# The output projection of one token block by seven products, and four reorderings around the norms

## The chip, the cores and the metric

The kernel runs on one core of a Trainium2 chip. The metric is device time in microseconds (us) of one execution; a time is the median of several runs. PE is the matrix engine, PEld its weight loads, DVE the vector engine, ACT the scalar engine, POOL GpSimd, and SP the engine that here only issues DMAs. ACT, DVE, SP and POOL each take their instructions in the order in which the kernel's program queues them.

## The reference

2112 tokens (2048 of a prompt, 64 of a sample) pass one layer, all in float32:

```
h = rms_norm(x, g_pre);  proj = h @ w_in                  # ten groups of 1024 columns
yA = (silu(zA) * bA * conv3(cA * vA)) @ w_a_out
o  = gated linear attention over chunks of 64 tokens (8 heads of 128)
yB = (rms(o) * g_onorm * silu(zB)) @ w_b_out
merged = sigmoid(gA) * yA + sigmoid(gB) * yB
out = merged @ w_o
x = x + rms_norm(out, g_post)
gate = sigmoid(rms_norm(x, g_ple) @ w_ple_gate)
x = x + (p @ w_ple_proj) * gate
```

## The kernel before

**Tiling.** The tokens are cut into three blocks (0, 1, 2) of 704, each with two halves ("segs") of 352. Activations lie features by tokens: a tile of 128 features x 704 tokens is a `rt()` of one ring of 52 tiles. A float32 product is made of three matmuls in a split format: each operand is cut into `hi` (an ACT cast) and `lo` (a DVE subtraction, `split`), and hi x hi, hi x lo and lo x hi are summed in PSUM. The low parts of the weights are written to DRAM the first time (`lows`, in `split_w`) and loaded later instead of computed.

**Seven products.** Most projections treat two blocks of output columns, two halves of the contraction and the two halves of tokens as a 2 x 2 block product in the Strassen-Winograd form: seven block products in place of eight, with sums of weight blocks (S1 to S4, kept in DRAM by `keep_sum` or `prepare_sums`) and of activation blocks (T1 to T4, `sums_of`). `sgroup` does so for one pair of columns. `in_turn` does it for a whole 1024 x 1024 matrix, one product after the other, each over four rows g of blocks (12 matmuls each); `operand_of` forms the next product's operand from the raw tiles, in place, one k after each row. Block 0 uses plain `gemms` for W_A, W_B and W_O. Block 1 uses `in_turn` for W_A and W_B (`merge_in_turn`) and `gemms` for W_O (`final_out`), for which `made` splits the merged tiles. Block 2 uses `in_turn` for all three (`out_in_turn`).

**The order of the work.** PE's work is written out as one sequence. Slower side work (norms, attention steps, operands) hangs on `hooks`, a list popped once after each product or row: `spread_out` says how many steps of a generator belong to each hook, and places them, on ACT and DVE, behind the latest PSUM evictions (`copies`, `adds`, by `behind_all`). `placed` puts matmuls of side work behind PE's last main matmul. Instructions are then put into each engine's queue by a scheduler that goes by priority and dependencies.

**PSUM.** Eight banks: five in `psg` (`ps_gemm`, written pg in the profile) and three in `psa` (`ps_attn`, written pa).

**Between blocks.** While W_O of block b is worked, `operands` scales the x of block b+1 and makes its seven operands, one k pair at a time. Then `gates` starts for block b+1: eight groups, seven of them (`LEAD`) at once, with block b's `final_norm` on their hooks: the root mean square (`rms`: column sums L614 on PE, a power on POOL L587, a broadcast L598 on PE, a copy on ACT L624), eight steps that make x, a second root mean square, and eight that make h. The eighth gate group is taken up by `path_b` at head 0. In the last block the norm runs by halves, on hooks of W_O, of the second projection `ple` (L1028 to L1030, evicted at L1035) and of the gate matmuls.

**The start.** Block 0's `ple` and its row sums come first; then `plain_group` takes k by k what `first_operands` has split, and between two k's `next_k` runs one operand step and one step of block 1's `ple` (`second_ple`).

Of the kernel before, what the change touches and what calls it, by code (L numbers as in the profile page):

```python
# [78 lines left out]
IN_TURN = (("A11", "B11"), ("A12", "B21"), ("S2", "T2"), ("S3", "T3"), ("A22", "T4"), ("S1", "T1"), ("S4", "B22"))  # L79
# [3 lines left out]
def hybrid_step(  # L83
# [113 lines left out]
    lows, turn = {}, [0]  # L197
# [11 lines left out]
    def split_w(raw, key=None):  # L209
# [9 lines left out]
        if key is not None:  # L219
            lows[key] = dram.tile([P, 4, P], F32, tag=f"lo{key}", name=nm("low"), bufs=1)  # L220
            SP.dma_start(lows[key], lo.bitcast(F32))
# [12 lines left out]
    last, hooks, copies, adds = [None], [], [None], [None]  # L234
# [33 lines left out]
    def keep_sum(name, i1, s):  # L268

        sums.setdefault(i1, {})[name] = dram.tile([P, 4, P], F32, tag=f"{name}_{i1}", name=nm(name), bufs=1)  # L270
        SP.dma_start(sums[i1][name], s)
        return split_w(s, (i1, name))
# [179 lines left out]
    def operand_of(raw, name, k):  # L452

        (b11, b12), (b21, b22) = ([half(raw[i], h) for h in range(2)] for i in (k, k + KH))
        if name == "T2":
            V.tensor_tensor(b11, b12, b11, ALU.subtract)
            t = hf()
            V.tensor_tensor(t, b22, b11, ALU.subtract)
            V.tensor_tensor(b12, b22, b12, ALU.subtract)
            V.tensor_tensor(b21, b21, t, ALU.subtract)  # L460
            return narrow(t)
        return narrow(dict(B11=b11, B21=b21, T3=b12, T4=b21, T1=b11, B22=b22)[name])

    def in_turn(stages, operand):

# [4 lines left out]
        def prepare(i, k):  # L470
            if i < len(todo):
                st, n = todo[i]
                made.setdefault(i, []).append(operand_of(st["raw"], IN_TURN[n][1], k))

        for i, (st, n) in enumerate(todo):
            if n == 0:
                st["mid"], st["bank"] = [], {}
            xs = made.pop(i)
            for g in range(KH):
                i1, i2 = st["idx"] + g, st["idx"] + KH + g  # L480
                with tc.high_priority():
                    hi, lo = kept_w(i1, i2, IN_TURN[n][0], IN_TURN[n][0] in st["anew"])
                start = n in (0, 2, 3, 5)
                if start:
                    st["bank"][g] = ps_gemm()
                ps = st["bank"][g]
# [6 lines left out]
                if n == 0:  # L493
# [3 lines left out]
                u2, p7 = half(st["mid"][g], 0), half(st["mid"][g], 1)  # L497
                if n == 1:
                    st["sink"](g, 0, 0, ps, None)
                elif n == 2:  # L500
                    V.tensor_tensor(u2, u2, ps, ALU.add)
                elif n == 3:
                    with tc.high_priority():
                        A.copy(p7, ps)
                elif n == 4:
                    st["sink"](g, 1, 0, u2, ps)
                elif n == 5:
                    p5 = hf()
                    with tc.high_priority():
                        A.copy(p5, ps)  # L510
                    V.tensor_tensor(p7, p7, p5, ALU.add)
                    st["sink"](g, 1, 1, u2, p7)
                elif n == 6:
                    st["sink"](g, 0, 1, u2, ps)
# [103 lines left out]
    def rms(acc, out, segs):  # L618
# [4 lines left out]
        for sg, col in zip(segs, cols):  # L623
            A.copy(out[:, cols_of(sg)], spread(col, sg["n"]))  # L624
# [56 lines left out]
    def operands(hc, rs, load):  # L681

        for i in range(KH):
            pair = []
            for k in (i, i + KH):
                pair.append(load(k))
                scaled_x(pair[-1], k, rs)
            hc["B11"].append(narrow(half(pair[0], 0)))
            sums_of(hc, pair)
            hi, lo = split_rt(pair[1])  # L690
            hc["B21"].append((half(hi, 0), half(lo, 0)))
            hc["B22"].append((half(hi, 1), half(lo, 1)))
            yield
# [292 lines left out]
    def path_b(bl, hc, first, kept, fills, hs):  # L986
# [25 lines left out]
    def ple(bl, ph, kept, held=None, shared=False):  # L1012

        for j in range(KB):
            if held is not None:
                hi, lo = held[j]
            else:
                raw = wp.tile([P, 4, P], F32, tag="raw", name=nm("raw"), bufs=5)[:, :2, :]
                SP.dma_start(raw, w_ple[j])
                with tc.high_priority():  # L1020
                    hi = wp.tile([P, 4, P], F32R, tag="hi", name=nm("hi"))[:, :2, :]
                    lo = wp.tile([P, 4, P], F32R, tag="lo", name=nm("lo"))[:, :2, :]
                    split(raw, hi, lo)
            t = rt()
            for s in bl["segs"]:
                pp, c = ps_attn()[:, :HN], cols_of(s)
# [11 lines left out]
            else:  # L1038
                kept["p", j] = spill("p", j)
                G.dma_start(kept["p", j], t)  # L1040
            with behind_all((copied,) if hooks else ()):
# [45 lines left out]
    def merge_in_turn(a, kept, mg, made):  # L1087
# [9 lines left out]
        def sink_b(g, c, h, x, y):  # L1097
# [3 lines left out]
            made(j, h)  # L1101

        def loads(idx, n):
# [13 lines left out]
            dict(idx=W_A, raw=a, sink=sink_a, anew=("A11", "A12")),  # L1117
            dict(idx=W_B, raw=ob, sink=sink_b, anew=("A11", "A12")),
        ], loads

    def final_out(segs, mg, xo, acc, late):

        for j, pss in enumerate(gemms(W_O, mg, segs, True, late)):
# [10 lines left out]
    def out_in_turn(mg, xo, acc):  # L1134
        xo.extend(rt() for _ in range(KB))
        begun = set()

        def sink(g, c, h, x, y):
            v = half(xo[g + c * KH], h)
            into(v, x, y)  # L1140
            sum_squares(int(h in begun), v, half(acc, h), HN)
            begun.add(h)

        return dict(idx=W_O, raw=mg, sink=sink, anew=())

    def final_norm(bl, segs, xo, acc, h2, kept):
# [15 lines left out]
        yield from rms(acc, rs, segs)  # L1162
        for j in range(KB):
# [4 lines left out]
            sum_squares(j, xj, acc2[:, c], n)  # L1168
            yield
        yield from rms(acc2, rs2, segs)  # L1170
        for j in range(KB):
            xj = xo[j][:, c]
# [5 lines left out]
            t = rt()  # L1178
            V.scalar_tensor_tensor(t[:, c], xj, g_ple[:, j : j + 1], rs2[:, c], ALU.mult, ALU.mult)
# [263 lines left out]
```

## Time and profile before

| | |
|---|---|
| median of 3 runs | 2653.56 us (2651.12 to 2655.82) |
| the profiled execution, its own time | 2661.89 us |
| its span, first to last instruction | 2660.2 us |
| mean clock granted to PE | 0.994 |
| DMA | 732.90 MB, mean 276 GB/s |
| HBM read, written | 524.66 MB, 205.01 MB |

How to read it: a busy share is an average over stages with different limits, so what an edit is worth is read in its stage. Matmuls are pipelined, and the duration of one (324 ns for 352 columns) is about twice the distance between two starts, so time is counted from start to start. Likewise DVE and ACT operations overlap their successors a little. A wait is put down to the releaser that came last.

### The profile page before, as it was taken

Reading aid. Unit: us, or ns where it says so; the run is one execution under the profiler, and the core shown is the slowest. Engines: PE = TensorE matmul, PEld = TensorE weight load, DVE = VectorE, ACT = ScalarE, POOL = GpSimd, SP = SyncE. Lnnn points to the kernel's source line nnn. Section 1 sums busy time; section 2 is a strip of 40 time slices with the busy share of each in tenths; the row PEclk is TensorE's granted clock in tenths of the full one; section 3 lists DMA queues with packets and bytes.
Section 4 is the critical chain, followed back from the end, with each engine's and each line's share of the span. In section 5 each row is a group of like instructions: output and inputs, shape, how many; then the busy total and the mean of one; then the engine's idle time right before and its main releaser. Section 6 shows DMA issues by size and latency. Waiting matters only on the chain.

```text
span 2660.2 us, 47727 instructions
## 1 busy us (share of the span) xinstructions
PE 2624.7 (99%) x16748; PEld 2606.2 (98%) x16748; DVE 1688.3 (63%) x3281; ACT 1474.9 (55%) x2872; POOL 351.3 (13%) x649
## 2 busy tenths in 40 slices
PE   7999999999999999999999999999999999999999
PEld 7999999999999999999999999999999999999998
DVE  7688888888676555556645577553365554347856
ACT  5665665554335544566655565554566654445664
POOL 1000000200441210101112210021000000001011
PEclk9999999999999999999999999999999999999999
DMA  7677787988997988676689988698866678889965
GB/s 288 218 275 271 247 281 259 314 310 289 373 348 268 352 299 270 225 230 221 223 290 363 389 308 290 191 349 312 273 218 220 216 227 264 273 277 313 298 210 177
DMA packets 359793, 732.90 MB, mean 276 GB/s; under 512 B 43808, under 2 KB 46400, under 8 KB 359552
## 3 DMA queue, kind: packets, MB, share of 16 engines
q1 hardware_dynamic: 322560, 586.10, 65.6%
q0 software_dynamic: 36704, 143.70, 14.9%
q8 instruction: 132, 2.16, 0.3%
q14 instruction: 109, 0.89, 0.1%
q10 hardware_dynamic: 288, 0.05, 0.0%
HBM read 524.66 MB, written 205.01 MB: 274 GB/s over the span
## 4 chain that ended last, share of the span: by engine, by line
PE 91%; DMA 3%; DVE 3%; issue 2%; ACT 1%; POOL 0%; SPq 0%; ACTq 0%; DVEq 0%; POOLq 0%
PE pg L357 19%; PE pg L359 19%; PE pg L358 19%; PE pg L525 5%; PE pg L523 5%; PE pg L524 5%; PE pg L491 3%; PE pg L490 3%; PE pg L492 3%; DMA raw<-S 2%; PE pa L963 1%; PE pa L927 1%; PE pa L917 1%; PE pa L965 1%; PE pa L916 1%
## 5 line engine op out<-in xcount | busy, mean ns | idle before, releaser
L357 PE MATMUL pg<-r,hi 128*128 128x352 f32 x3304 | 1094.0, 331 | 1.9 <-ACT hi L214 1.5
L358 PE MATMUL pg<-r,hi 128*128 128x352 f32 x3304 | 1069.1, 324 | 0.0
L359 PE MATMUL pg<-r,lo 128*128 128x352 f32 x2356 | 763.0, 324 | 3.7 <-DMA lo<-low 3.7
L214 ACT CAST hi<-raw 128x512 fp32r<-128x512 f32 x708 | 435.5, 619 | 572.6 <-PE pg L358 202.0
L357 PEld LDWEIGHTS pg<-r,hi 128*128 128x128 f32 x3304 | 623.6, 189 | 6.1 <-issue 2.2
L358 PEld LDWEIGHTS pg<-r,hi 128*128 128x128 f32 x3304 | 623.5, 189 | 0.1
L359 PEld LDWEIGHTS pg<-r,lo 128*128 128x128 f32 x2356 | 444.0, 188 | 4.4 <-DMA lo<-low 4.3
L359 PE MATMUL pg<-r,s 128*128 128x352 f32 x948 | 307.3, 324 | 2.4 <-DMA s<-low 2.4
L524 PE MATMUL pg<-r,hi 128*128 128x352 f32 x896 | 289.8, 324 | 0.4 <-DVE r L184 0.4
L523 PE MATMUL pg<-r,hi 128*128 128x352 f32 x896 | 289.7, 324 | 0.4 <-ACT r L184 0.3
L525 PE MATMUL pg<-r,lo 128*128 128x352 f32 x756 | 244.6, 324 | 0.1
L184 ACT CAST hi<-raw 128x512 fp32r<-128x512 f32 (+1 forms) x242 | 145.8, 612 | 163.8 <-PE pg L358 45.5
L184 DVE TENSOR_TENSOR r<-r,r 128x352 fp32r<-128x352 f32 (+3 forms) x274 | 169.5, 636 | 65.6 <-ACT r L184 64.9
L184 DVE TENSOR_TENSOR lo<-raw,hi 128x512 fp32r<-128x512 f32 (+1 forms) x242 | 162.7, 678 | 72.9 <-ACT hi L184 61.3
L184 ACT CAST r<-r 128x352 fp32r<-128x352 f32 (+3 forms) x274 | 150.3, 578 | 67.5 <-DVE r L666 17.5
L491 PE MATMUL pg<-r,hi 128*128 128x352 f32 x560 | 181.9, 325 | 0.4 <-DVE r L184 0.3
L359 PEld LDWEIGHTS pg<-r,s 128*128 128x128 f32 x948 | 178.7, 189 | 3.2 <-DMA s<-low 3.2
L490 PE MATMUL pg<-r,hi 128*128 128x352 f32 x560 | 178.5, 325 | 0.1
L184 ACT CAST hi<-s 128x512 fp32r<-128x512 f32 x160 | 99.0, 619 | 139.0 <-PE pg L358 119.7
L523 PEld LDWEIGHTS pg<-r,hi 128*128 128x128 f32 x896 | 168.7, 188 | 1.4 <-ACT r L184 1.1
L524 PEld LDWEIGHTS pg<-r,hi 128*128 128x128 f32 x896 | 168.8, 188 | 0.8 <-DVE r L184 0.6
L371 ACT COPY hf<-pg 128x352 f32<-128x352 f32 x354 | 155.8, 448 | 6.8 <-PE pg L359 6.3
(365 smaller groups left out, 4088.4 us busy)
## 6 DMA issues: line engine op xcount, KB each, us to landing
raw<-w_blk SPq DMA_DIRECT2D x590, 256.0 KB, 3.9
lo<-low SPq DMA_DIRECT2D x404, 256.0 KB, 3.9
raw<-S SPq DMA_DIRECT2D x392, 256.0 KB, 4.0
low<-lo SPq DMA_DIRECT2D x346, 256.0 KB, 3.7
s<-low SPq DMA_DIRECT2D x304, 256.0 KB, 3.9
S<-s SPq DMA_DIRECT2D x160, 256.0 KB, 3.3
r<-w_blk POOLq DMA_DIRECT2D x48, 256.0 KB, 7.5
S<-r POOLq DMA_DIRECT2D x48, 256.0 KB, 6.2
```

What stands on the lines that cost most here:

```text
L184: return A.copy(hi, src).ins, V.tensor_tensor(lo, src, hi.bitcast(F32), ALU.subtract).ins
L214: A.copy(hi, raw)
L357: add(hi[:, k, :], xhi, start=start and k == 0, stop=False)
L358: add(hi[:, k, :], xlo, start=False, stop=False)
L359: last[0] = add(lo[:, k, :], xhi, start=False, stop=k == KH - 1).ins
L371: copied = A.copy(got[n], ps[bank])
L490: add(hi[:, k, :], xhi, start=start and k == 0, stop=False)
L491: add(hi[:, k, :], xlo, start=False, stop=False)
L492: last[0] = add(lo[:, k, :], xhi, start=False, stop=k == KH - 1).ins
L523: T.matmul(ps, hi[:, k % 4, :], xhi[:, c], start=k == ks[0], stop=False)
L524: T.matmul(ps, hi[:, k % 4, :], xlo[:, c], start=False, stop=False)
L525: last[0] = T.matmul(ps, lo[:, k % 4, :], xhi[:, c], start=False, stop=k == ks[-1]).ins
```

## The change

1. W_O of block 1 goes through `in_turn` with an order of its own (`IN_TURN_LATE`): S1 T1 comes third, then S2 T2 into a bank of `psa`, S4 B22, S3 T3, A22 T4. `made` and its splits go. The squares of its output are taken in `final_norm`, on hooks of the gates.
2. `operands` has three steps for a pair in place of one and asks for the next pair's x ahead (`early`); they hang on the 28 hooks of that W_O.
3. From block 1 on the stores of sums and low parts are issued by POOL. The eighth gate group is taken up at head 4.
4. At the start `next_k` runs the projection ahead of the operand step, two steps of it the first time; the operand step goes behind the evictions, and three of `second_ple`'s halves use `ps_gemm`.
5. In the last block the squares of x lag by one tile, h's scalings run one tile ahead of its splits, the broadcasts are copied by DVE (`hasten`), the low parts of `w_ple` are loaded from DRAM, the last product's additions go behind that copy (`ahead`), and the counts of steps per hook change. Block 0's counts change as well.

```diff
+IN_TURN_LATE = (
+    ("A11", "B11", "p1"), ("A12", "B21", "c11"), ("S1", "T1", "p5"), ("S2", "T2", "u2"), ("S4", "B22", "c12"),
+    ("S3", "T3", "p7"), ("A22", "T4", "c21"),
+)
...
-            SP.dma_start(lows[key], lo.bitcast(F32))
+            stores[0].dma_start(lows[key], lo.bitcast(F32))
...
-        SP.dma_start(sums[i1][name], s)
+        stores[0].dma_start(sums[i1][name], s)
...
                 if start:
-                    st["bank"][g] = ps_gemm()
-                ps = st["bank"][g]
+                    other = what == "u2" and st["order"] is IN_TURN_LATE
+                    st["bank"][g] = [ps_attn()[:, :HN] if other else ps_gemm(), st["bank"].get(g)]
+                ps, held = st["bank"][g]
...
+            if hasten:
+                ahead[:] = [V.tensor_copy(out[:, cols_of(sg)], spread(col, sg["n"])).ins]
+            else:
+                A.copy(out[:, cols_of(sg)], spread(col, sg["n"]))
...
-    def operands(hc, rs, load):
+    def operands(hc, rs, load, early=False):
+        pair = None
         for i in range(KH):
-            pair = []
-            for k in (i, i + KH):
-                pair.append(load(k))
-                scaled_x(pair[-1], k, rs)
+            pair = pair or [load(k) for k in (i, i + KH)]
+            for k, xk in zip((i, i + KH), pair):
+                scaled_x(xk, k, rs)
             hc["B11"].append(narrow(half(pair[0], 0)))
+            yield
             sums_of(hc, pair)
+            yield
...
+            pair = [load(k) for k in (i + 1, i + 1 + KH)] if early and i + 1 < KH else None
             yield
...
-            if not (first and hd == 0):
+            if hd > 0 if first else hd == NH // 2:
                 next(fills, None)
...
-                    lo = wp.tile([P, 4, P], F32R, tag="lo", name=nm("lo"))[:, :2, :]
-                    split(raw, hi, lo)
+                    lo = low_tile()[:, :2, :]
+                    A.copy(hi, raw)
+                    SP.dma_start(lo.bitcast(F32), lows["p", j])
...
-                pp, c = ps_attn()[:, :HN], cols_of(s)
+                pp = ps_gemm() if spare and j in (1, 3, 5) and s is bl["segs"][1] else ps_attn()[:, :HN]
...
+        if squares:
+            for j in range(KB):
+                sum_squares(j, xo[j], acc, BN)
+                if j % 2:
+                    yield
...
-            sum_squares(j, xj, acc2[:, c], n)
+            for i in (j,) if not bl["last"] else (j - 1,) if 0 < j < KB - 1 else (j - 1, j) if j else ():
+                sum_squares(i, xo[i][:, c], acc2[:, c], n)
...
     def next_k():
-        run(ops, 1)
         with placed():
-            run(second_ple, 1)
+            run(second_ple, 2 if len(hs) == 2 else 1)
+        with behind_all(copies):
+            run(ops, 1)
...
+        if bi == 1:
+            stores[0] = G
...
+            stages.append(out_in_turn(mg, xo, acc, bl["last"]))
...
+                if nxt and (idx, n) == (W_B, 6):
+                    hc = new_operands()
+                    ops = operands(hc, spread_all(cols), partial(load_x, nxt), True)
+                    spread_out((ops, (0, 1, 0, 1, 0, 1, 0) * KH))
...
-                    spread_out((norms[0], (0, 0, 1, 0, 1, 1, 1, 1)))
+                    spread_out((norms[0], (1, 0, 1, 1, 1, 0, 1, 0)))
...
-            spread_out((norm, (0, 1, 0, 1) + (0, 1, 0) * KB + (1, 0, 1) + (0, 1) * KB))
+            start = (0, 1, 0, 1) + (0, 1, 0) * KB if first else (1, 1, 1, 1, 0, 1, 0, 1) + (0, 1) * KB
+            spread_out((norm, start + (0, 1, 0, 1) + (0, 1) * KB))
...
-            spread_out((norms[0], (2, 2, 1, 1, 1, 3, 3, 2)), (norms[1], (0,) * 6 + (1, 1) + (2, 2, 2, 2, 1, 0, 1, 3, 3, 2)))
+            spread_out((norms[0], (2, 2, 1, 0, 1, 1, 4, 4)), (norms[1], (0,) * 6 + (1, 1) + (1, 2, 2, 2, 1, 1, 1, 3, 3, 2)))
```

More of the change, by code (lines that the diff above doesn't have):

```diff
@@ L231, in load_w @@
         return parts
-    last, hooks, copies, adds = [None], [], [None], [None]
+    last, hooks, copies, adds, ahead = [None], [], [None], [None], []
     def placed():
@@ L1132, in final_out, with out_in_turn, final_norm @@
         yield
-    def out_in_turn(mg, xo, acc):
-        xo.extend(rt() for _ in range(KB))
+    def out_in_turn(mg, xo, acc, last):
+        stage = dict(idx=W_O, order=IN_TURN if last else IN_TURN_LATE, raw=mg, anew=())
+        if last:
+            xo.extend(rt() for _ in range(KB))
         begun = set()
         def sink(g, c, h, x, y):
-            v = half(xo[g + c * KH], h)
+            if not last and c == 0 and h == 0:
+                xo.append(rt())
+            v = half((xo if last or c == 0 else stage["mid"])[g + c * KH * last], h)
             into(v, x, y)
[L1141 to L1146, printed above, removed]
+            if last:
+                sum_squares(int(h in begun), v, half(acc, h), HN)
+                begun.add(h)
+        stage["sink"] = sink
+        return stage
+    def final_norm(bl, segs, xo, acc, h2, kept, squares=False):
         c = slice(segs[0]["off"], segs[-1]["off"] + HN)
```

134 lines of the change are left out of this document (74 added, 60 removed).

## The prediction

> **What bounds the kernel now.** I read the page's busy table and chain, then busy time by stage, then the matmul queue's waits stage by stage.
>
> ```profile
> span 2660.2 us, 47727 instructions
> PE 2624.7 (99%) x16748; PEld 2606.2 (98%) x16748; DVE 1688.3 (63%) x3281; ACT 1474.9 (55%) x2872; POOL 351.3 (13%) x649
> ...
> PE 91%; DMA 3%; DVE 3%; issue 2%; ACT 1%; POOL 0%; SPq 0%; ACTq 0%; DVEq 0%; POOLq 0%
> ```
>
> PE is busy for 99% of the span and is 91% of the chain. A matmul not issued is therefore worth its pitch, and besides that only the places count where PE is held up or runs at a lower clock. The stages (columns: stretch, length, then PE, PEld, DVE, ACT, POOL busy, PE clock, DMA share, GB/s):
>
> ```profile
> 33.00:36.50 3.50, 3.50 (x14) 3.27 (x13) 3.50 (x6) 1.58 (x5) 0.00 (x0) 0.52 1.04 410
> ...
> 57.00:61.00 4.00, 4.00 (x17) 4.00 (x16) 3.42 (x6) 1.10 (x3) 0.33 (x1) 0.57 0.93 300
> 920.50:924.00 3.50, 3.50 (x15) 3.50 (x14) 0.00 (x0) 0.99 (x3) 1.51 (x2) 0.52 1.05 401
> 1064.00:1067.50 3.50, 3.50 (x14) 3.50 (x13) 0.52 (x1) 1.41 (x2) 0.00 (x0) 0.51 0.70 249
> ...
> 1591.00:1646.00 55.00, 54.90 (x334) 53.34 (x333) 46.00 (x101) 34.70 (x75) 5.33 (x10) 1.00 0.89 301
> 1646.00:1661.00 15.00, 14.33 (x90) 13.38 (x89) 12.15 (x27) 5.93 (x13) 1.60 (x3) 1.00 0.80 296
> 1661.00:1722.00 61.00, 61.00 (x381) 61.00 (x380) 29.35 (x43) 28.82 (x52) 3.75 (x7) 1.00 0.58 186
> 1722.00:1785.00 63.00, 59.54 (x366) 58.18 (x366) 32.69 (x51) 38.90 (x71) 14.22 (x24) 0.97 0.97 351
> ...
> 2441.00:2495.00 54.00, 54.00 (x335) 53.59 (x334) 47.15 (x100) 34.33 (x75) 7.44 (x14) 1.00 0.95 332
> 2570.00:2576.00 6.00, 5.92 (x20) 5.92 (x21) 5.93 (x15) 4.19 (x12) 0.00 (x0) 0.50 0.18 44
> ```
>
> The undisturbed stage 2441 to 2495 gives the pitch: 54.00 us / 335 matmuls = 0.161 us for 352 columns. At clock 0.51, 14 matmuls filled 3.5 us, 0.25 us each; a half-clock stretch of about 3.4 us thus costs 3.4 x (1 - 0.161/0.25), 1.2 us, to 3.4/2 = 1.7 us. I use 1.5.
>
> PE's hold-ups that the change can reach (the bracket is the idle time and its releaser):
>
> ```profile
> 30.06 0.81 PE L427 MATMUL pg<-r,hi 128*128 128x352 f32 x2 [1.22 <-ACT r L184]
> 32.17 0.43 PE L428 MATMUL pg<-r,hi 128*128 128x352 f32 x1 [1.30 <-DVE r L184]
> 50.11 0.43 PE L1028 MATMUL pa<-r,r 128*128 128x352 f32 x1 [1.75 <-ACT r L1035]
> 56.19 0.43 PE L1028 MATMUL pa<-r,r 128*128 128x352 f32 x1 [1.96 <-ACT r L1035]
> ...
> 1063.19 0.43 PE L359 MATMUL pg<-r,lo 128*128 128x352 f32 x1 [2.25 <-DMA lo<-low]
> ...
> 1656.46 0.43 PE L523 MATMUL pg<-r,hi 128*128 128x352 f32 x1 [0.27 <-ACT r L184]
> 1657.24 0.43 PE L524 MATMUL pg<-r,hi 128*128 128x352 f32 x1 [0.36 <-DVE r L184]
> ...
> 1723.05 0.43 PE L357 MATMUL pg<-r,hi 128*128 128x352 f32 x1 [0.75 <-ACT hi L214]
> ...
> 2570.08 0.66 PE L1028 MATMUL pa<-r,hi 128*128 128x352 f32 x1 [3.77 <-ACT r L1035]
> ...
> 2608.12 0.83 PE L614 MATMUL pa<-ones,r 128*128 128x1 f32 x6 [0.25 <-DVE r L633]
> 2610.39 1.65 PE L598 MATMUL pa<-ident,cols 128*128 128x128 f32 x6 [1.44 <-POOL cols L587]
> ```
>
> And PE's waits summed for 1715 to 1785, the gates of block 2 with block 1's norm between them:
>
> ```profile
> PE pg L359 <- DMA s<-low: 1.5, 1, 1.5
> PE pa L614 <- DVE r L633: 1.2, 1, 1.2
> PE pg L357 <- ACT hi L214: 0.7, 1, 0.7
> ```
>
> **The change, part by part.** The sum is made against the profiled execution, 2661.89 us (span 2660.2), 8.3 us or 0.3% above the median 2653.56; I carry the difference over to the median.
>
> *a. Matmuls of W_O in block 1.* Before: 8 columns x 2 halves x 8 k x 3 = 384. After: 7 products x 4 rows x 4 k x 3 = 336. 48 x 0.161 = **-7.7 us**. The sums of W_O's blocks are written in block 1 already, so nothing is added ahead.
>
> *b. That stage's own load.* Its weights become 28 raw and 28 low tiles instead of 16 and 16: 56 x 256 KB in 54 us is 271 GB/s, and the eight x tiles for block 2 (128 x 704 x 4 bytes, 0.36 MB each) add 53, together 324. The stage 2441:2495 moved 332 with PE busy for 54.00 of 54.00, so DMA has a cover. DVE is nearer its limit. Its starts:
>
> ```profile
> 1644.06 0.52 DVE L184 TENSOR_TENSOR r<-r,r 128x352 fp32r<-128x352 f32 x1
> 1644.49 0.52 DVE L1092 TENSOR_TENSOR r<-hf,r 128x352 f32<-128x352 f32 x1
> ```
>
> are 0.435 us apart for 352 columns (I take 0.80 for 704, 0.86 for scaled x). Per row of blocks a stage of seven products has 6 operand splits (the first is made in the stage before), 4 sums for the T's and 5 evictions: 4 x 15 x 0.435 = 26 us. Block 2's operands are 4 pairs of 2 x 0.86 + 5 x 0.435 + 3 x 0.80 = 6.3, 25 us. Together 51 of 54 us, without order counted. W_B's stage loses the 16 half splits that `made` put there (7 us of DVE). Its DVE was busy for 46.0 of 55 and then 12.15 of 15 us, the queue that makes W_O's first operands late at 1656. That loss of 1.5 us with pipeline refill goes: **-1.2** (bounds -1.5, and +4 if DVE runs behind). Small waits inside such a stage: **+1.3**, the nearest row being the 0.6 us at 1656 twice over (bounds 0 and +6). The entry to the gates at 1723, where the last pair came late, gives **-0.8** (bounds -1.0 and +3); its pair is now issued within the stage, by the 27th of 28 hooks.
>
> *c. Block 1's squares move behind the gates' first products.* 8 x (0.80 DVE + about 0.7 ACT) must end before the column sums (L614), which are queued in PE's order from the sixth hook, about 11 us after the gates begin; hidden if DVE arrives without a backlog. The x steps come every two hooks instead of three, DMA there is at 0.97 already and the waits of 1.5 and 1.2 us and the slower clock stay likely: **+1.0** (bounds -4, all of them gone with a half-clock stretch, and +5, each doubled).
>
> *d. Block 0's norm* gets a hook more (1.93 us, 12 matmuls) before its second column sums, ahead of the half-clock stretch at 920: **-1.2** (bounds -2.3 and +1). Its other waits are for weights and stay.
>
> *e. The last gate group of block 1* moves from head 0 to head 4, and the stores of sums and low parts from SP's queue to POOL's. Before, loads stand behind stores:
>
> ```profile
> 1043.63 0.38 SPq L271 DMA_DIRECT2D S<-s  x1
> 1049.07 0.33 SPq L194 DMA_DIRECT2D raw<-S  x1
> 1049.68 0.32 SPq L221 DMA_DIRECT2D low<-lo  x1
> ```
>
> SP issues nothing for 5.4 us, and the low tile is late at 1063 by 2.25 us, with a half-clock stretch behind it. On POOL the stores have gate spills, and the attention's power operations, behind them, none due within a group. 2.25 + 0.4 + 1.5 = 4.2 at most: **-3.5** (bounds -4.2, and +3 if the group starves at head 4 as well).
>
> *f. The last block's tail.* ACT holds three squares, each waiting for DVE's newest x, ahead of the eviction that frees PE's bank:
>
> ```profile
> 2566.89 0.88 ACT L632 ACTIVATE r<-r 128x352 f32<-128x352 f32 x2 [1.06 <-DVE r L1167]
> 2569.19 0.50 ACT L632 ACTIVATE r<-r 128x352 f32<-128x352 f32 x1 [1.41 <-DVE r L1167]
> 2569.59 0.79 ACT L1035 COPY r<-pa 128x352 f32<-128x352 f32 x2
> ```
>
> The squares now lag by one, the norm starts two hooks earlier, the low parts of w_ple are loaded instead of computed, and h's scalings run one ahead. At stake are 3.77 us and, at clock 0.50, about 2.7 of the 6 us behind it; then 0.25 + 1.44 and a second stretch of 1.3 at 2611. What is late next is DVE: 8 x 3 operations for the first half's x alone are 11 us, and the earlier column sums can themselves stop PE. I take about half, **-5.5** (bounds -9.5 and +3).
>
> *g. The start.* PE waits 1.22 + 1.30 for the first split, then 1.75 and 1.96 for banks held by ACT, with two half-clock stretches (33 and 57): 9.2 us. Two steps of the second projection now run ahead, and three of its halves take the fifth bank of the other pool. The next limit is DVE's last split:
>
> ```profile
> 57.21 0.89 DVE L184 TENSOR_TENSOR r<-r,r 128x704 fp32r<-128x704 f32 x1 [0.33 <-ACT r L184]
> ...
> 66.97 0.32 PE L427 MATMUL pg<-r,hi 128*128 128x352 f32 x1
> ```
>
> It ends at 58.1 and PE uses it at 66.97 at the latest, so up to 8.9 us can go; splits now queued behind evictions take some back: **-4.5** (bounds -8.9 and +2).
>
> Sum: -7.7 - 1.2 + 1.3 - 0.8 + 1.0 - 1.2 - 3.5 - 5.5 - 4.5 = **-22.1 us**, or 2631.5 us from the median.
>
> On the clock the trace and a page differ. Here half-clock stretches follow waits of 1.96 us (57) and 2.25 us (1064). The Trainium skill, "TensorE: Matmul & The Clock Gate", section "Why this matters for your kernels", says instead to keep idle gaps under some 3 us, since one idle window brings the half clock back. By that rule only the gap at 2570 carries its stretch, and e and g would give about 4 us less in all, -18 us; by the rows a shorter wait that goes takes its stretch with it, and the sum above is by the rows.
>
> **The rivals.**
> *Only the matmuls count.* The stalls reappear one engine further on: DVE at the tail (5.93 of 6.00 us busy at 2570), DVE at the start (3.50 of 3.50 at 33), DMA in the gates (0.97). Then -7.7 with some 0 to -4 of e, about -8: 2645.5. Against it: at 50 and 56 PE waited for a bank, not for a split.
> *No difference.* The seven products save their 7.7 us and lose them in their own stage, where DVE goes from 29 of 61 us to 51 of 54, while the tail and the start give 3 and c takes 3: 2653.
> *Slower.* One mechanism: in W_O's stage block 2's operand work, in chunks of 6.3 us in DVE's order, stands ahead of the evictions and splits that the next product needs. If none of its 25 us is hidden, and each of the seven products then also pays a half-clock stretch of 1.5, that is +36: with the -22 of the rest 2667. It decides over slower once the stage loses more than 27 us, about 4 per product. Against it: the three steps per pair are placed at separate hooks, and each operand has a product (7.7 us) of lead.
>
> **How the numbers follow.** The forecast (-12 to -33) has 0.62; matmuls only (-5.3 to -12) 0.20; no difference 0.09; slower 0.05; more than -33, with f and g near their ends, 0.04. A measurement here can tell about 0.2%, 5.3 us, from no change. Faster: 0.62 + 0.20 + 0.04 = 0.86. The range takes the first two, -33.5 to -5.5: 2620 to 2648. The two signs are not both likely, so one range stands.
>
> **What would show it.** a: 336 matmuls between W_B's last product and the gates, in 54 to 56 us. b: DVE at about 50 of 54 us there, PE without idle of more than 0.5. c: L614 of block 1's norm waiting for L633 by more than 1.2 us speaks for the first rival. e: no wait near 1060, and none of that size at head 4. f: no wait for L1035 at the last projection, and PE clock 1.0 behind it. g: L1028 not waiting for L1035 before 70 us, and the plain group ended before 80. The prediction is wrong if the W_O stage takes over 62 us, or if the stalls at the start and the tail are as long as before under other names.

## The result and the profile after

The changed kernel took 2640.41 us (median of 6 runs, 2637.55 to 2645.6) against 2654.69 for the kernel before on the same chip (6 runs, 2651.12 to 2659.43): ratio 0.9949, 95% interval 0.9935 to 0.9963, or 14.3 us less. Two later measurements gave 0.9936 (0.9921 to 0.9952) and 0.9937 (0.9923 to 0.9951). The three ratios put the gain at 13 to 17 us, about 16. The forecast was 22.1.

The page of the changed kernel's profiled execution (2640.08 us, at the median of its runs):

```profile
span 2638.4 us, 47798 instructions
...
PE 2610.8 (99%) x16700; PEld 2593.0 (98%) x16700; DVE 1708.9 (65%) x3325; ACT 1483.9 (56%) x2892; POOL 360.0 (14%) x665
```

There are 48 matmuls fewer, as counted. Three stretches of it, W_O of block 1, the gates behind it and the last block's tail (length, then PE, PEld, DVE, ACT, POOL busy, PE clock, DMA share, GB/s):

```profile
1644.50:1702.10 57.60, 56.42 (x340) 53.97 (x339) 50.47 (x97) 40.54 (x84) 4.28 (x8) 1.00 0.86 290
...
1702.10:1807.40 105.30, 102.38 (x637) 101.51 (x637) 58.49 (x88) 66.62 (x120) 17.68 (x31) 0.98 0.95 339
2548.40:2633.00 84.60, 82.44 (x515) 80.46 (x514) 63.17 (x131) 48.39 (x105) 13.63 (x23) 1.00 0.66 211
```

The same three in the kernel before:

```profile
1652.10:1715.55 63.45, 62.78 (x388) 61.83 (x387) 33.84 (x54) 29.91 (x56) 4.68 (x9) 1.00 0.59 190
...
1715.55:1821.70 106.15, 102.69 (x637) 101.33 (x637) 56.04 (x86) 64.49 (x119) 17.53 (x30) 0.98 0.93 332
2563.25:2655.10 91.85, 86.39 (x517) 85.45 (x516) 65.27 (x135) 49.54 (x106) 13.65 (x23) 0.94 0.57 180
```

W_O is 5.9 us shorter, the gates 0.9, the tail 7.1 (from its first matmul to its last). PE's hold-ups that are left in the parts touched by the change, without those for loads, from the changed kernel's timeline (L1062 to L1064 and L1069 are the old L1028 to L1030 and L1035, L192 the old L184, L366 to L368 the old L357 to L359, L637 the old L614, L621 the old L598, L659 the old L633):

```profile
56.69 0.43 PE L1062 MATMUL pa<-r,r 128*128 128x352 f32 x1 [3.22 <-ACT r L1069]
97.12 0.44 PE L937 MATMUL pa<-ident,r 128*128 128x128 f32 x2 [1.78 <-DVE r L412]
1494.76 0.40 PE L366 MATMUL pg<-r,hi 128*128 128x352 f32 x1 [0.20 <-DVE hf L386]
1497.56 0.40 PE L366 MATMUL pg<-r,hi 128*128 128x352 f32 x1 [0.61 <-DVE r L412]
1660.42 0.59 PE L511 MATMUL pg<-r,hi 128*128 128x352 f32 x2 [0.18 <-ACT r L192]
1673.95 0.74 PE L511 MATMUL pa<-r,hi 128*128 128x352 f32 x3 [0.39 <-ACT r L192]
1674.93 0.43 PE L512 MATMUL pa<-r,hi 128*128 128x352 f32 x1 [0.24 <-DVE r L192]
1721.84 1.50 PE L637 MATMUL pa<-ones,r 128*128 128x1 f32 x12 [0.15 <-DVE r L659]
2551.58 0.43 PE L1062 MATMUL pa<-r,hi 128*128 128x352 f32 x1 [0.15 <-ACT r L1069]
2554.19 0.43 PE L1062 MATMUL pa<-r,hi 128*128 128x352 f32 x1 [0.42 <-ACT r L1069]
2559.35 0.43 PE L1062 MATMUL pa<-r,hi 128*128 128x352 f32 x1 [0.61 <-ACT r L1069]
2591.39 0.94 PE L621 MATMUL pa<-ident,cols 128*128 128x128 f32 x6 [0.83 <-POOL cols L610]
```

The 3.77 us of the tail have become waits of 0.15 to 0.61, and nothing stands at 1060. At the start the waits for the first splits and the two for banks became one of 3.22 for a bank. In the gates of block 2 PE still waits for loads, as before, while the wait for the column sums is down from 1.2 us to 0.15 and the one for a cast is gone; summed over these gates:

```profile
PE pg L368 <- DMA lo<-low: 1.9, 1, 1.9
PE pg L368 <- DMA s<-low: 0.8, 1, 0.8
PE pa L637 <- DVE r L659: 0.2, 1, 0.2
```

Stage lengths in us, each from the first matmul of one stage to the first of the next in the rows of the traces (two profiles of the kernel before, three of the changed one; the stages left out, block 0's and block 1's last gate and block 2 up to its last projection, do not change by more than 0.9 us):

| stage | before | changed |
|---|---|---|
| start | 77.5, 76.5 | 71.7, 73.1, 71.8 |
| block 0: paths and plain projections | 770.6, 771.9 | 775.3, 770.2, 770.7 |
| gates with block 0's norm | 106.5, 102.9 | 102.6, 101.7, 103.6 |
| block 1: paths | 517.7, 519.8 | 516.0, 516.5, 517.2 |
| block 1: W_A, W_B, W_O | 174.6, 173.9 | 167.7, 167.6, 168.4 |
| gates with block 1's norm | 106.2, 103.0 | 105.3, 104.4, 103.8 |
| last projection to last matmul | 91.9, 90.0 | 84.8, 84.9, 84.8 |

### The profile page after: what moved, and what is told of

The parts are those of the page before. It is cut to its first block, busy times and chain, and to the rows that moved or that the text cites. A ratio compares the mean times of both kernels' runs of the same rounds, so it can differ in the third digit from the quotient of the medians.

```text
span 2638.4 us, 47798 instructions
## 1 busy us (share of the span) xinstructions
PE 2610.8 (99%) x16700; PEld 2593.0 (98%) x16700; DVE 1708.9 (65%) x3325; ACT 1483.9 (56%) x2892; POOL 360.0 (14%) x665
## 5 line engine op out<-in xcount | busy, mean ns | idle before, releaser
L366 PE MATMUL pg<-r,hi 128*128 128x352 f32 x3304 | 1095.3, 332 | 1.9 <-ACT hi L222 0.7
L368 PE MATMUL pg<-r,lo 128*128 128x352 f32 x2356 | 763.2, 324 | 2.8 <-DMA lo<-low 2.8
L222 ACT CAST hi<-raw 128x512 fp32r<-128x512 f32 x720 | 443.0, 620 | 569.8 <-PE pg L367 204.9
L366 PEld LDWEIGHTS pg<-r,hi 128*128 128x128 f32 x3304 | 622.8, 189 | 5.9 <-issue 3.7
L367 PEld LDWEIGHTS pg<-r,hi 128*128 128x128 f32 x3304 | 623.1, 189 | 0.0
L368 PEld LDWEIGHTS pg<-r,lo 128*128 128x128 f32 x2356 | 444.0, 188 | 3.5 <-DMA lo<-low 3.5
L368 PE MATMUL pg<-r,s 128*128 128x352 f32 x948 | 306.7, 323 | 0.8 <-DMA s<-low 0.8
L192 ACT CAST hi<-raw 128x512 fp32r<-128x512 f32 x234 | 142.6, 619 | 160.3 <-PE pg L367 44.5
L548 PE MATMUL pg<-r,lo 128*128 128x352 f32 x688 | 222.5, 323 | 0.3 <-DVE lo L192 0.2
L192 DVE TENSOR_TENSOR r<-r,r 128x352 fp32r<-128x352 f32 (+3 forms) x282 | 173.2, 633 | 54.6 <-ACT r L192 53.6
L192 DVE TENSOR_TENSOR lo<-raw,hi 128x512 fp32r<-128x512 f32 x234 | 159.2, 686 | 68.3 <-ACT hi L192 55.3
L192 ACT CAST r<-r 128x352 fp32r<-128x352 f32 (+3 forms) x282 | 153.2, 576 | 50.1 <-DVE r L692 15.1
L368 PEld LDWEIGHTS pg<-r,s 128*128 128x128 f32 x948 | 178.3, 188 | 1.2 <-DMA s<-low 1.1
L192 ACT CAST hi<-s 128x512 fp32r<-128x512 f32 x160 | 99.1, 619 | 141.9 <-PE pg L367 115.5
L546 PEld LDWEIGHTS pg<-r,hi 128*128 128x128 f32 x768 | 144.2, 188 | 1.2 <-ACT hi L192 0.8
L547 PEld LDWEIGHTS pg<-r,hi 128*128 128x128 f32 x768 | 144.3, 188 | 0.7 <-DVE r L192 0.6
```

Of the source, the lines that this page charges most:

```text
L192: return A.copy(hi, src).ins, V.tensor_tensor(lo, src, hi.bitcast(F32), ALU.subtract).ins
L222: A.copy(hi, raw)
L366: add(hi[:, k, :], xhi, start=start and k == 0, stop=False)
L367: add(hi[:, k, :], xlo, start=False, stop=False)
L368: last[0] = add(lo[:, k, :], xhi, start=False, stop=k == KH - 1).ins
L546: T.matmul(ps, hi[:, k % 4, :], xhi[:, c], start=k == ks[0], stop=False)
```

## The experiments

Theory: each part gains what its own stage loses in the table, the parts add up, and the difference of 6 us to the forecast lies in the profiled execution of before, which was a long one. Rival one: the parts give back elsewhere what they gain. Rival two: the new W_O stage is bound by DVE and costs what the sides gain.

**Both kernels once more**, unaltered.

> The kernel before, unchanged, profiled once more. Theory A: the profiled execution that the prediction read (2661.89 us) was a high one, 7 us over the median of 2654.69, and part of the 21.8 us between the two traces was never in the usual execution. Then this profile comes out at 2651 to 2658 us, with fewer half-clock stretches than the seven between 30 and 2615 us, and single stages (the start, 77.5 us; the last block's tail from the second projection on, 91.9 us; block 0's gates, 106.5 us) are shorter than there by 1.5 us or more each. Rival B: that trace was typical, and the profile adds time of its own: then again about 2661 us, every stage within 0.5 us. Ratio of the times to before: 1.000 by both, which also shows the noise.

> The changed kernel, unchanged, timed on the same chip as the parts. Both theories: ratio 0.9935 to 0.9963 as measured before. Theory A: its stages stay within 1 us of the first trace's (start 71.7, block 0's gates 102.6, W_A to W_O of block 1 167.7, tail 84.8 us), since it ran without most half-clock stretches. Rival B': this kernel varies as much as the one before, and the first trace was a lucky one: then some stage is longer by 3 us or more.

Measured: 2658.04 (10 runs, 2652.03 to 2663.22; ratio 1.0006, 0.9995 to 1.0018) and 2639.21 (6 runs). The profiled execution of the first took 2653.91 us, 8.0 less than the one that the prediction was made from, with the same program. By the table two of the three stages named are shorter by more than 1.5 us, the start only by 1.0, and block 1's paths are 2.1 longer. The changed kernel's start came out 1.4 us longer than in its first profile and block 0's paths and plain projections 5.1 shorter, so that first profile was not a lucky one. The page of the profiled execution of before_again and, from its timeline and its stretches, two of its waits and the clock behind the second:

```profile
span 2652.2 us, 47727 instructions
...
60.82 0.42 PE L1028 MATMUL pa<-r,r 128*128 128x352 f32 x1 [1.81 <-ACT r L1035]
...
2603.88 0.93 PE L598 MATMUL pa<-ident,cols 128*128 128x128 f32 x6 [1.45 <-POOL cols L587]
...
2604.00:2608.00 4.00, 4.00 (x27) 4.00 (x28) 4.00 (x10) 1.55 (x4) 2.63 (x5) 1.00 0.58 207
```

The wait of 1.45 us for L587 stands in both profiles of before (1.44 at 2610 in the first). There the six matmuls of the broadcast behind it took 1.65 us and the clock halved; here they took 0.93 at clock 1.00. The first profile holds seven half-clock stretches, one of them double, this one three. That is four or five times 1.5, 6 to 7.5 of the 8 us.

**W_O alone, and all but W_O.** wo_only is the kernel before with `IN_TURN_LATE`, `out_in_turn` for block 1, `operands` in three steps and the squares in `final_norm`; the start, the stores, the eighth gate group, the counts of block 0 and of the last block, and the tail are as before. wo_undone is the reverse (its main lines):

```diff
-                if nxt and (idx, n) == (W_B, 6):
-                    hc = new_operands()
-                    ops = operands(hc, spread_all(cols), partial(load_x, nxt), True)
-                    spread_out((ops, (0, 1, 0, 1, 0, 1, 0) * KH))
...
-            stages.append(out_in_turn(mg, xo, acc, bl["last"]))
+            if not nxt:
+                stages.append(out_in_turn(mg, xo, acc, bl["last"]))
```

> The kernel before with the seven products of W_O in block 1 alone (their order, operands in three steps, x asked ahead, squares on the gates' hooks); the start, the tail, the stores, the gate group at head 0 and block 0's counts as before. Theory A (the matmuls count fully, the rest of the stage gives and takes little): W_A to W_O of block 1 about 167.7 us against 174.6, and 6 to 9 us less in time, ratio 0.9966 to 0.9977. Rival (the stage's DVE load and the squares behind it take most of it back): under 3 us, ratio over 0.9989.

> The changed kernel with W_O of block 1 by plain products as before, all else of the change kept. Theory A: 6 to 9 us more than the changed kernel, ratio to before 0.997 to 0.9985, so that the start, the tail, the stores and the counts are together worth 5 to 8 us in time and not the 13.7 us of the prediction's sum (d, e, f, g and -0.8 + 1.0 of b and c). Rival: they are worth 12 us or more, ratio 0.9955 or less, and W_O gives little.

Measured, against 2655.19: wo_only 2647.72 (12 runs; 0.9972, 0.9959 to 0.9985), 7.5 us less; wo_undone 2644.16 (6 runs; 0.9953, 0.994 to 0.9967), 11.0 less. For wo_only this is what was expected. For wo_undone it is not: 5 to 8 us were expected of the rest, and the 11.0 lie nearer to the rival's 12, though W_O does not give little, as that rival had it. Together 18.5, and the whole change 16.0, measured beside them: the parts add up within the 3 to 4 us that an interval is wide on either side. W_O's stage in wo_only:

```profile
1647.55:1705.00 57.45, 56.33 (x339) 54.00 (x339) 50.53 (x97) 40.53 (x84) 4.28 (x8) 1.00 0.84 291
```

It is that of the changed kernel to 0.2 us, DVE busy for 50.5 us included. W_A to W_O takes 167.4 us in it, against 174.6 and 173.9 in the kernel before. The stage gains about 6 us by itself, so rival two falls.

**The start put back.**

```diff
-    second_ple = ple(blocks[1], ph, kepts[1], held, spare=True)
+    second_ple = ple(blocks[1], ph, kepts[1], held)
...
+        run(ops, 1)
         with placed():
-            run(second_ple, 2 if len(hs) == 2 else 1)
-        with behind_all(copies):
-            run(ops, 1)
+            run(second_ple, 1)
```

> The changed kernel with the start alone put back (one step of the second projection after each operand step, its halves all in the three banks of psa). Stages theory (the gain of a part is the time that its own stage loses, and nothing is given back elsewhere): the start goes from about 72 to 76.5 us, of which 1 us comes back at block 0's first transposes, which wait 1.9 us for DVE in the changed kernel and 0.8 in the one before; so 2640 becomes 2643 to 2645, 0.995 to 0.997 of the kernel before. Rival (the start's gain is given back in block 0's paths, where the changed kernel took 586.2 in one profile): within 1 us of the changed kernel, 0.994. No change elsewhere: tail 84.8, W_O stage 55 with 336 matmuls.

Measured 2643.56 (5 runs; 0.9952, 0.9937 to 0.9967). The start takes 77.8 us, 1.3 more than the stages theory had. Three waits for a bank stand there, and the one at the first transposes stays:

```profile
50.29 0.43 PE L1062 MATMUL pa<-r,r 128*128 128x352 f32 x1 [1.99 <-ACT r L1069]
56.37 0.43 PE L1062 MATMUL pa<-r,r 128*128 128x352 f32 x1 [1.95 <-ACT r L1069]
62.13 0.43 PE L1062 MATMUL pa<-r,r 128*128 128x352 f32 x1 [1.63 <-ACT r L1069]
...
103.03 0.44 PE L937 MATMUL pa<-ident,r 128*128 128x128 f32 x2 [1.79 <-DVE r L412]
```

So the wait at the transposes is no gift back of the start, as I had expected: it is 0.6 to 1.8 us in the fourteen profiles and varies with the execution. In the four where it is 1.78 or 1.79 a half-clock stretch follows, and block 0's paths and plain projections take 775.3 to 777.9 us; in the ten others they take 769.6 to 773.2. This kernel, with the old start, is one of the four. The part is worth 3 us by the medians, which the intervals do not separate from the changed kernel's, and 5 to 6 us by the stage's length.

**The tail put back** (squares, h's scalings, broadcasts, w_ple's low parts and the last block's counts).

```diff
-        yield from rms(acc, rs, segs, bl["last"])
+        yield from rms(acc, rs, segs)
...
-            for i in (j,) if not bl["last"] else (j - 1,) if 0 < j < KB - 1 else (j - 1, j) if j else ():
+            for i in (j,):
...
-                    SP.dma_start(lo.bitcast(F32), lows["p", j])
+                    split(raw, hi, lo)
```

> The changed kernel with the last block's tail put back (squares not lagging, the copies of the broadcasts on ACT, old counts of steps per hook, the low parts of w_ple computed). Stages theory: the tail (last projection to the last matmul) goes from 84.8 back to 89.7 to 90 us, so the time is 4 to 5.5 us above the changed kernel, 2644 to 2646, 0.996 of the kernel before. In the profile the wait of 3.8 to 4 us of L1062 (the projection's first matmul) for ACT's eviction returns, and the two behind it (0.25 to 0.4 and 1.4 to 1.6). Rival (the tail gains only the half-clock stretch that one profile showed behind its wait): 2641 to 2642.

Measured 2645.25 (6 runs; 0.9961, 0.9946 to 0.9975), about 5 us above the changed kernel by the medians, in the part of the range that I gave the stages theory; the interval reaches down to that of the changed kernel. The tail is 89.8 us again, and PE's two waits are back:

```profile
2550.56 0.43 PE L1061 MATMUL pa<-r,hi 128*128 128x352 f32 x1 [3.79 <-ACT r L1068]
...
2590.37 0.93 PE L621 MATMUL pa<-ident,cols 128*128 128x128 f32 x6 [1.45 <-POOL cols L610]
```

**Stores, eighth gate group and block 0's counts put back.**

```diff
-            stores[0] = G
+            stores[0] = SP
...
-            if hd > 0 if first else hd == NH // 2:
+            if not (first and hd == 0):
...
-            spread_out((norm, start + (0, 1, 0, 1) + (0, 1) * KB))
+            spread_out((norm, start + ((1, 0, 1) if first else (0, 1, 0, 1)) + (0, 1) * KB))
```

> The changed kernel with the stores back on SP's queue, the eighth gate group at head 0 and block 0's old counts of steps per hook. Stages theory: the waits near 1060 return (2.2 to 3.6 us, with 1.4 of half clock behind them), and the smaller s and lo waits in the paths of block 1 (1437 to 1498) that the changed kernel has instead, 1 to 2.9 us, go: net 2 to 4 us above the changed kernel, 2642 to 2644, 0.995 to 0.996 of the kernel before. Rival (the waits of loads are only moved, whichever queue issues the stores): within 1 us of the changed kernel.

Measured 2641.16 (6 runs; 0.994, 0.9924 to 0.9955): the rival's side. The waits near 1060 are back, without half clock this time:

```profile
1050.95 0.40 PE L366 MATMUL pg<-r,hi 128*128 128x352 f32 x1 [0.75 <-DVE hf L386]
1060.53 0.43 PE L368 MATMUL pg<-r,lo 128*128 128x352 f32 x1 [1.24 <-DMA lo<-low]
```

and those at 1494 and 1497 are gone. The paths of block 1 take 516.8 us, inside the 516.0 to 517.2 of the changed kernel. In the four profiles with the gate group at head 0 PE's waits there come to 1.9 to 3.2 us, with a half-clock stretch behind them in two; at head 4, in ten profiles, to at most 1.6 us, mostly about 1, and never with a stretch. What the move can win is thus 1 to 2 us and, in some executions, a stretch. This kernel also has block 0's old counts: its gates with block 0's norm take 103.2 us, inside the 101.7 to 103.6 of the changed kernel.

**x on every third hook.** Block 1's norm in the gates of block 2, over the same 44 hooks:

```diff
-            start = (0, 1, 0, 1) + (0, 1, 0) * KB if first else (1, 1, 1, 1, 0, 1, 0, 1) + (0, 1) * KB
-            spread_out((norm, start + (0, 1, 0, 1) + (0, 1) * KB))
+            start = (0, 1, 0, 1) + (0, 1, 0) * KB if first else (1, 1, 1, 1, 0, 1, 0, 1) + (0, 1, 0) * KB
+            spread_out((norm, start + (0, 1, 0, 1) + ((0, 1) * KB if first else (1,) * KB)))
```

> The changed kernel with block 1's norm spread otherwise over the same 44 hooks of the gates: its eight x steps every three hooks instead of every two, and its eight h steps one per hook instead of every second. If the steps' loads cause the wait of 2.1 us for a low tile near 1745 and the half clock behind it (DMA is at 0.97 there), it shrinks below 0.5 and the gates take 102 to 103 us instead of 104.4 to 105.3: 2637 to 2639, 0.993 of the kernel before. Rival (the loads of the gates' own weights are the cause, or h in single hooks makes the last products wait for DVE): same as the changed kernel within 1 us, or up to 3 us slower with a wait of path_a for h at the end of the gates.

Measured 2634.33 (5 runs; 0.992, 0.9905 to 0.9936), some 3 us below what I expected. The gates take 102.7 us, as the theory had it, and the wait for a low tile is 0.72, not below 0.5. In the changed kernel's three profiles it is 1.95, 0.99 and 1.06, so that the one that the expectation read was the longest:

```profile
1748.78 0.43 PE L368 MATMUL pg<-r,lo 128*128 128x352 f32 x1 [0.72 <-DMA lo<-low]
...
1704.65:1807.30 102.65, 100.92 (x637) 99.96 (x637) 58.05 (x88) 66.22 (x120) 17.66 (x31) 1.00 0.97 349
```

The nine profiles with W_O in turn and x on every second hook have 103.8 to 105.3 there. The edit moves more than the x steps' loads (the h steps come closer together), so that the loads are the cause is likely, not shown.

**A bank more at the start, and the operand steps elsewhere.**

```diff
-                pp = ps_gemm() if spare and j in (1, 3, 5) and s is bl["segs"][1] else ps_attn()[:, :HN]
+                pp = ps_gemm() if spare and j in (1, 3, 5, 6) and s is bl["segs"][1] else ps_attn()[:, :HN]
```

> The changed kernel, whose second projection takes the fifth bank of the other pool for one half more, that of tile 6. In the changed kernel PE stands 3.4 us near 53 at the second half of this tile, for a bank that ACT empties behind two casts that wait for DVE, and 1.5 to 3 us of half clock follow. Bank theory (the bank is what it lacks; the spare one is empty since 51.4): the wait goes, and the next limit is the split for the last plain steps, so the start takes 67 to 69 us in place of 71.7 to 73.1: 2635 to 2637, 0.993 of the kernel before. Rival (DVE's splits are the bound of the start, as the first rival of the prediction had it): the same 3 us turn up as a wait of the plain group for the split, the start stays at 71 to 73 us, and the time at 2639 to 2640.

```diff
-                    spread_out((ops, (0, 1, 0, 1, 0, 1, 0) * KH))
+                    spread_out((ops, (0, 1, 0, 1, 0, 1, 0, 1) + (0,) * 4 + (1, 0) * 8))
```

> The changed kernel with block 2's operand steps on other hooks of block 1's W_O: none in the four rows in which T2, the longest operand (three subtractions and a split), is made, and the other eight every second hook behind them. If DVE's order is what holds PE in the product S2 T2 (waits of 0.3, 0.55, 0.39 us and smaller ones between 1670 and 1677), these go and W_A to W_O takes 165.5 to 166.5 us in place of 167.6 (block 2's takes 165.1): 1 to 2 us, 2638 to 2639. Rival (the waits are those of T2's own chain of subtraction, cast and subtraction over DVE and ACT): they stay, and 167.6 with them; with the last pair's steps as late as before, the first product of the gates waits as in the changed kernel (1.0 us).

Measured beside each other: spare_six 2636.59 (6 runs; 0.992, 0.9905 to 0.9935), steps_off_t2 2639.2 (6 runs; 0.993, 0.9915 to 0.9945). In the first the wait of 3.22 us is gone, and smaller ones stand in its place. The last of them is for a bank again: ACT empties it with the gates' sigmoid, behind the load of the sigmoid's table (PE's rows, then ACT's):

```profile
52.47 0.43 PE L1062 MATMUL pg<-r,r 128*128 128x352 f32 x1 [1.40 <-ACT r L1069]
60.15 0.43 PE L437 MATMUL pg<-r,hi 128*128 128x352 f32 x1 [0.31 <-DVE r L192]
67.23 0.43 PE L436 MATMUL pg<-r,hi 128*128 128x352 f32 x1 [1.34 <-ACT r L755]
...
65.42 1.28 ACT L755 ACT_TABLE_LOAD   x1
66.71 0.82 ACT L755 ACTIVATE r<-pg 128x352 f32<-128x352 f32 x2
```

The start takes 72.3 us, as the rival had it, but not by the rival's mechanism: only 0.31 us of PE's waits behind 50 us are for a split, 2.74 for banks. Another 1.54 us is a wait for the first split, at 32.12, which none of the changed kernel's three profiles has and two_joined, with the same bank, lacks too; two_joined's start takes 70.6 us. Without that wait both lie about 1 us or more below the 71.7 to 73.1 of the changed kernel, and PE's largest wait there is still for a bank. The time is what the bank theory gave; no half-clock stretch is left between the first matmul of that execution and its last. In the second kernel the wait has moved to the head of the same product and is longer:

```profile
1665.66 0.75 PE L511 MATMUL pa<-r,hi 128*128 128x352 f32 x3 [1.58 <-ACT r L192]
```

W_A to W_O takes 167.3 us, within 0.4 of two of the changed kernel's. With no operand step in the rows where T2 is made, the product S2 T2 still waits: this speaks for T2's own chain as the cause, against the operand steps in DVE's queue.

**Both gains together**, with the changed kernel beside it.

> The changed kernel, unaltered, as the measure for the kernel with two edits beside it on the same chip: 2639 to 2641, 0.993 to 0.995 of the kernel before.

> The changed kernel with both edits: the x steps of block 1's norm on every third hook and its h steps on every hook (gates 102.7 us in place of 104.4 to 105.3), and the spare bank for tile 6 at the start (no half-clock stretch there; 0 to 3 us). Stages theory: 2 to 4 us below the changed kernel, 2635 to 2637. Rival (the 2634 seen with the x steps alone was spread between runs): within 1 us of the changed kernel's time in the same call.

Measured: the changed kernel 2636.99 (6 runs), 2 us lower than expected, two_joined 2634.78 (6 runs, 2632.38 to 2638.92; 0.9926, 0.9914 to 0.9939). It is the shortest of the kernels but x_every_three, whose median was 0.5 lower on another chip; 2.2 us to the changed kernel is within the intervals, so in time this gain is not settled. Its gates, from its stretches, show where it lies:

```profile
1697.85:1798.70 100.85, 100.71 (x637) 100.05 (x637) 58.16 (x88) 66.37 (x120) 17.68 (x31) 1.00 0.97 351
```

PE is busy for all but 0.14 of them, against 2.9 us idle in the changed kernel's first profile.

**The fourteen profiles by part.** In time most parts are no larger than the intervals. The lengths of the stages separate three of them: each profile here belongs to the side whose edit its kernel has (us; the number of profiles in brackets).

| stage, and its part of the change | without | with |
|---|---|---|
| start | 76.4 to 77.8 (4) | 70.6 to 73.1 (10) |
| gates with block 0's norm, its counts | 102.9 to 106.5 (4) | 101.7 to 103.6 (10) |
| block 1: paths, stores and eighth gate group | 515.8 to 519.8 (4) | 514.8 to 517.9 (10) |
| block 1: W_A, W_B, W_O, in turn | 173.9 to 174.6 (3) | 167.3 to 168.4 (11) |
| gates with block 1's norm, W_O in turn and x on every second hook | 102.3 to 106.2 (3) | 103.8 to 105.3 (9) |
| last projection to last matmul | 89.7 to 91.9 (4) | 84.8 to 85.3 (10) |

For the start, W_O and the tail no profile of one side reaches the other; the means differ by 4.9, 6.4 and 5.3 us, 16.6 together. The other three overlap (two profiles with x on every third hook are left out of them), with means 2.1 and 1.1 us shorter and 0.5 us longer.

## Why the prediction came out as it did

The direction and the range held, and so did the mechanisms of a, c, f and most of g: 2640.4 lies in 2620 to 2648, 8.9 us above the point. The step that failed is "I carry the difference over to the median", and with it "a shorter wait that goes takes its stretch with it". Both take one execution's stalls for those of every execution. The profiled one lay some 6 us above the median of the kernel before in the five later measurements (2654.7 to 2656.8) and held seven half-clock stretches, where the second profile of the same program held three.

That the two profiled executions differ by 21.8 us (2661.89 to 2640.08), where the forecast was 22.1, is luck. In the table's first columns the six stages that the change touches fall by 26.3 us together, and block 0's paths and plain projections rise by 4.7, with the wait of 1.78 us at the first transposes. The profiles of the table differ by 20.6 us in the mean, the medians by 16, so the sizes measured below are some 4 to 5 us too large in all. The nine terms against the table (means of the columns):

- a and b, W_O's stage and the one ahead: -7.6 forecast, -6.3 measured. The matmuls went as counted, but not "in 54 to 56 us": W_O's stage took 57.6, 57.5 and 58.3. "DVE at about 50 of 54 us" came out at 50.5 of 57.6. The small waits are the term that was too small: hold-ups of over 0.08 us beyond the pitch add up to 3.4 us, half of it in S2 T2, where 1.3 was allowed. The entry to the gates (-0.8) gave nothing: PE waited 0.75 for a cast before, 0.82 for a sum's load after.
- c, the squares behind the gates: hidden, as forecast. L637 waits 0.15 us, where the first rival wanted more than 1.2. The gates stayed the same within 0.1 us, against +0.2 with the entry; over all profiles they are 0.5 us longer. With the x steps on every third hook they took 102.7 and 100.9 us, 1.7 and 3.5 below the mean of the nine others.
- d: -1.2 forecast, -2.1 by the table and over the fourteen profiles, but those with the old counts spread over 3.6 us and sides_undone shows no loss, so the size stays open.
- e: -3.5 forecast. The table says -2.2, the fourteen profiles -1.1, and the experiment that undoes it, together with d, 0 to 1 us in time. "2.25 + 0.4 + 1.5" took the half-clock stretch for certain, and "none due within a group" left out that the group at head 4 waits for DVE's evictions instead.
- f: -5.5 forecast, -6.1 measured, 5.3 over the fourteen profiles, 5 by the experiment. Right, with the clock at 1.00 behind it; of "no wait for L1035" three waits of 0.15 to 0.61 us are left.
- g: -4.5 forecast, -4.8 measured, 4.9 over the fourteen profiles, 3 by the experiment. The size held, but the sign "L1028 not waiting for L1035 before 70 us" was wrong: one wait of 3.22 us for that bank is left, with the half clock behind it. "The next limit is DVE's last split" did not hold either: in spare_six PE waits 2.74 us for banks and 0.31 for a split.

The first rival (2645.5) is refuted by wo_undone: without any matmul saved the rest is worth 11 us. No difference is refuted too: W_O's stage keeps about 6 of its 7.7 us, and start and tail give 10. So is the slower one: W_O's stage lost 3.4 us to waits, not 27.

## What to carry to other kernels

Before a sum is made against a profiled execution, see how far that execution lies from the median; if it is above, some of its stalls belong to that execution alone, and a gain worked out from them has to be scaled down by as much. Where parts are no larger than the spread between runs, compare the lengths of their stages over several profiles. A seven-product stage with DVE at 88% of its span still gains; the largest part of what it loses here lies in the operand with the longest chain. Where PE runs into loads at a DMA share of 0.95, other hooks for the side work shortened the stage by 1.7 and 3.5 us, one profile each, while moving the stores to another engine's queue gained nothing that the times show.

## What was not expected of the hardware

The price of one and the same wait varies from execution to execution. Over the fourteen profiles I counted PE's waits beyond the pitch (from start to start, so 0.16 us more than in the brackets) and looked for a half-clock stretch that begins within 1.5 us before to 3.5 us after their end: 12 of 12 waits of 3.37 to 3.97 us have one, 10 of 17 of 1.9 to 2.8 us, 6 of 25 of 1.25 to 1.9 us, some of these in the reach of a neighbouring wait. Every stretch between the first matmul and the last lasts 3.4 or 6.8 us. The one behind the wait at 56.69 in the changed kernel:

```profile
57.90:61.40 3.50, 3.50 (x15) 3.50 (x14) 3.20 (x6) 0.78 (x1) 0.00 (x0) 0.51 0.91 298
```

The Trainium skill, "TensorE: Matmul & The Clock Gate", section "Why this matters for your kernels", asks to keep idle gaps under some 3 us. Above that the traces agree. Below it they do not: waits of about 2 us cost a stretch in about half the cases.

The traces' clock records show what decides. Within each trace the starts of the stretches lie whole multiples of 3.413 us apart. So each trace can be cut into windows of 3.413 us, and for each window one can add up how long PE had no matmul to start (each matmul of 352 columns counted with its pitch of 0.161 us). Of 7019 windows at full clock with no narrower matmul in them, the 20 with 2.1 us or more without work are all followed by a half-clock window, and none of the 6999 others is; the emptiest of these lacks 1.95 us. What counts is thus how much of a wait falls into one window. A wait of 2 to 3 us costs a stretch if it falls mostly into one and nothing if a boundary cuts it, and where the boundaries lie differs between executions. In windows with column sums, broadcasts or transposes a stretch follows more easily (8 of 3675, the least with 0.87 us without work); why is open. The two waits for L587 are of this kind: the one of 1.44 us falls into one window, which lacks 1.86 us in all, the one of 1.45 us is cut by a boundary, and neither window lacks more than 1.4.

So neither the -18 us, with stretches behind gaps of over 3 us alone, nor the -22 by the first trace's rows counts rightly: before a run a wait between 2 and 3 us has only a chance of costing a stretch.
